# Low parts of second weight halves made by accumulating transfers

## The chip, the core and the metric

The kernel runs on one core of a Trainium2 chip. The time is device microseconds of one execution; the kernel before was timed twice, and 426.48 us is the median of the two (426.15 and 426.8). A profiled execution of its own gives the trace that is read below. "Within 2%" of the median is 418.0 to 435.0 us.

## The reference

One pre-norm residual layer on 512 tokens of width 1024, in float32, with two parallel token mixers that share one input projection:

```
h = rmsnorm(x, norm_g)
(q_lat, c_kv, k_rope, z_a, q_b, k_b, v_b, z_b,
 q_idx, k_idx, w_idx, gate_a, gate_b) = split(h @ w_in)
y_a = latent_attention(q_lat, c_kv, k_rope) * silu(z_a)      # 8 heads, chunk-causal softmax
y_b = topk_attention(q_b, k_b, v_b, q_idx, ...) * silu(z_b)  # 8 heads, an indexer keeps 128 keys
merged = sigmoid(gate_a) * (y_a @ w_o_a) + sigmoid(gate_b) * (y_b @ w_o_b)
x = x + merged @ w_out
return rmsnorm(x, final_g)
```

Nearly all the work is matrix products of activations with weights that are read once from HBM.

## The kernel before

**Products in three terms.** Every float32 operand `v` of a product is held as two tiles of the matmul type fp32r: a high part `hi`, which is `v` rounded to that type, and a low part `lo = v - hi`. A product of two such pairs is three matmuls, `hi*hi`, `hi*lo` and `lo*hi` (`mm3`, line 443; the matmul itself is recorded at line 438). A weight tile therefore costs, before TensorE can use it, a cast on ScalarE (line 331) and a subtraction on VectorE (line 362) or GpSimd (line 364).

**Jobs.** The projections are a list of jobs, in the order of the table `QUEUE`. One job loads one raw weight block into one of four buffers `raw0` to `raw3` (128 partitions, up to 1024 floats, 512 KB), and multiplies it. Three threads walk through the list: `fetcher` issues the load on SyncE's queue (line 465) as soon as a raw buffer is free; `splitter` makes the high and low parts, one half of 512 columns after the other (`split_w`); `multiplier` issues the matmuls, into accumulators of which at most three may be held by products at one time. `ga0` to `ga7`, `gb6`, `gb7` (gates), `za0` to `zb3` (SiLU paths) and the blocks `w_kb` and `w_qb` of `sb0` to `sb3` (keys and queries of the second mixer) are jobs of two halves of 512 columns each: 26 jobs. Names in capitals in the table go through a Strassen-like scheme and split their weights elsewhere.

**Slots.** High and low parts live in slots of 128x512 floats. `WCAP` bounds how many slots the class `w` may hold at one time: 8, that is, four halves. A half's two slots come free when TensorE has read them for the last time. The early weights of `early_w` (the key-value latent and the indexer, line 665 on) are under the same bound.

**The planner.** The order on each engine is not written out. `Flow` (line 151 on) runs while the program is built: some fifty threads (jobs, heads, softmaxes) each offer one step; the planner holds an estimate of each step's length and of each tile's readiness, and takes the step that would start first, ties and near ties going by priority. A step of `BOTH` engines goes to VectorE or GpSimd, whichever would end first. So an edit of one step's engine or estimate moves the order of everything behind it. Each engine then executes its own list strictly in order, and a wait holds up all that stands behind it. `multiplier` has the last priority but one (`PFILL`): its products fill TensorE between the steps of the attention heads.

**Heads.** A head's logits are four tiles of 128, 256, 384 and 512 keys (lines 1532 to 1534, three matmuls each, in the first mixer), written into two accumulator banks in turn (class `lg`, at most two held). A bank is free for the next tile when VectorE has taken its row maxima (line 1517) and ScalarE its exponentials with their sums (line 340). Softmax scaling, transposes (line 455) and the product with the values follow. The operands of the logits are put together by small transfers on SyncE's queue (`qhi`, `s_op`).

**GpSimd's own queue of transfers** (`pool_dma`, line 469) carries constants and small tables only, 15 transfers in the first 80 us.

Of the kernel before, what the change touches and what calls it, by code (L numbers as in the profile page):

```python
# [14 lines left out]
AF = mybir.ActivationFunctionType  # L15
ALU = mybir.AluOpType
# [4 lines left out]
S = 512  # L21
# [118 lines left out]
def put(*bufs):  # L140
    for b in bufs:
        b.home.used[b.cls] -= 1
        b.home.free.append(b)
# [7 lines left out]
class Flow:  # L151
# [16 lines left out]
    def spawn(self, gen, prio):  # L168
        t = Thread(gen, prio)
        self.threads.append(t)  # L170
        self.advance(t, None)
        return t
# [107 lines left out]
def tile_block(ctx: ExitStack, tc: tile.TileContext, a: dict, out: bass.AP, bias_dram: bass.AP):  # L280
    nc = tc.nc
# [28 lines left out]
    def in_ps(v):  # L310
        return id(v.buf) in ps_bufs

    def slot(cls, cap=None):
        return Get(SB, cls, cap)
# [8 lines left out]
    def bufs(*vs):  # L323
        return [v.buf for v in vs if isinstance(v, View)]
# [19 lines left out]
    def act(dst, src, func=AF.Copy, scale=None, bias=None, accum=None):  # L344
        step = Step([act_opt(dst, src, func, scale, bias, accum)], bufs(dst, accum), bufs(src, scale, bias))
        step.count = 2 if accum is not None else 1
        return step

    def rounded_by_dve(dst, src):
        step = Step([("DVE", 0.1 + 0.00052 * src.n, lambda: nc.vector.tensor_copy(dst.ap, src.ap))], bufs(dst), bufs(src))  # L350
        step.pair = True
        return step

    def soon(step):
        step.pbias = 0.0
        return step

    def tt(dst, x, y, op, engs=("DVE",)):
        opts = []
        for e in engs:  # L360
            if e == "DVE":
                opts.append(("DVE", 0.07 + 0.00104 * x.n, lambda: nc.vector.tensor_tensor(dst.ap, x.ap, y.ap, op=op)))  # L362
            else:
                opts.append(("POOL", 0.15 + 0.0021 * x.n, lambda: nc.gpsimd.tensor_tensor(dst.ap, x.ap, y.ap, op=op)))  # L364
        step = Step(opts, bufs(dst), bufs(x, y))
        step.pair = not (in_ps(x) or in_ps(y))
        return step
# [48 lines left out]
    def lo_part(lo, x, hi, engs=BOTH):  # L416

        return tt(lo, x, hi.f, ALU.subtract, ("DVE",) if in_ps(x) else engs)
# [48 lines left out]
    def pool_dma(dst, src):  # L467
# [3 lines left out]
        step.moves = 4.0 * dst.n * dst.ap.shape[0] / 360000  # L471
        yield step

    def act_dma(dst, src):
        step = Step([("ACT", 0.06, lambda: nc.scalar.dma_start(dst.ap, src))], bufs(dst), [])
        step.moves = 4.0 * dst.n * dst.ap.shape[0] / 360000
        return step
# [158 lines left out]

    rbc = []

    def split_w(raw, w, dst, key, cls="w", cap=None, release=False, early=False):

        hi = yield slot(cls, cap)
        lo = yield slot(cls, cap)
        yield rounded_by_dve(hi[:, :w], raw) if key == FIRST and early else act(hi[:, :w], raw)
        step = lo_part(lo[:, :w], raw, hi[:, :w])
        yield soon(step) if early else step
        if release:
            put(raw.buf)
        dst[key] = (hi, lo)
# [16 lines left out]
    def early_w():  # L665
        for k in range(NK):
            yield Until(lambda: ("q", k) in eraw)
            raw, last = eraw["q", k]
            yield from split_w(raw, 256, ewq, k if k else FIRST, "w", WCAP, last, True)
            if k == 0:  # L670
                ewq[0] = ewq.pop(FIRST)
            yield Until(lambda: ("kv", k) in eraw)
            raw, last = eraw["kv", k]
            yield from split_w(raw, 328, ewkv, k, "w", WCAP, last, True)
        for k in range(NK):
# [184 lines left out]
    def topk(i):  # L860
# [11 lines left out]
        if i == NT - 1:  # L872

            flow.pbias = LATE

# [33 lines left out]
    class Job:  # L909
        def __init__(self, src, widths, body, cls="w", cap=None, prep=None):  # L910
            self.src, self.widths, self.body, self.raw, self.parts, self.cls, self.cap = src, widths, body, None, {}, cls, cap or WCAP
            self.prep = prep
            jobs.append(self)
# [11 lines left out]
    def splitter():  # L925
        for job in jobs:
            yield Until(lambda: job.raw is not None)
            if job.prep:
                if job.body:
                    yield from job.prep(job)  # L930
                else:
                    spawn(job.prep(job), 9)
                continue
            for p, w in enumerate(job.widths):
                o = sum(job.widths[:p])
                yield from split_w(job.raw[:, o : o + w], w, job.parts, p, job.cls, job.cap, p == len(job.widths) - 1)

    def multiplier():
        for job in jobs:
# [28 lines left out]
    def input_sums():  # L968

        yield Until(lambda: sums_due[0] in done)  # L970
        for k in range(4):
            f = []
            for i in (k, k + 4):
                if i in held:
                    f.append(held[i])
                    continue
                t = yield slot("tmp", TCAP)
                yield soon(tt(t.all.f, hT[i][0].all.f, hT[i][1].all.f, ALU.add, BOTH))
                f.append(t)
            x, y = (t.all.f for t in f)  # L980
            yield soon(tt(x[:, HI], x[:, LO], x[:, HI], ALU.subtract, BOTH))
            yield soon(tt(y[:, HI], y[:, HI], x[:, HI], ALU.subtract, BOTH))
            yield soon(tt(x[:, LO], y[:, HI], x[:, LO], ALU.add, BOTH))
            yield soon(tt(y[:, LO], y[:, LO], y[:, HI], ALU.subtract, BOTH))
            for i in range(2):
                hi = yield slot("hs")
                lo = yield slot("hs")
                yield act(hi.all, f[i].all.f)
                yield soon(lo_part(lo.all, f[i].all.f, hi.all))
                put(f[i])  # L990
                hs[k, i] = (hi, lo)
# [434 lines left out]
    class Pair:  # L1426
# [3 lines left out]
        w = property(lambda self: max(self.hi.w, self.lo.w))  # L1430
# [209 lines left out]
    def y_gate(br, j):  # L1640

        name = "w_za" if br == "a" else "w_zb"
        y = ya if br == "a" else yb
        yield Until(lambda: (br, 2 * j) in done and (br, 2 * j + 1) in done and (name, j) in zt)
        z = zt[name, j]
        yield tt(y[j].all.f, y[j].all.f, z.all.f, ALU.mult, BOTH)
        put(z)
        yield is_done("pairs")
        hi = yield slot("ys")
        lo = yield slot("ys")  # L1650
        yield from split_scaled(hi.all, lo.all, y[j].all.f, 0.5)
        put(y[j])
        ysplit[br, j] = (hi, lo)
# [336 lines left out]
    spawn(bias_table(), 5)  # L1990
    spawn(fetcher(), 9)
    spawn(splitter(), 9)
    spawn(multiplier(), PFILL)
    spawn(setup_last(), 10)
# [5 lines left out]
    for br in "ab":  # L2000
        for j in range(4):
            spawn(y_gate(br, j), 8)
    spawn(input_sums(), PSUMS)
    spawn(fetch_gates(), 9)
# [12 lines left out]
XAT = 3  # L2017
QPOOL = 0
PHCAP = 4
WCAP = 8  # L2020
TCAP = 5
PTOPK = 12.0
PSCORE = 13.0
# [3 lines left out]
ORDER = [0,1,2,3]  # L2027
QUEUE = 'ga0 ga1 pe ma0 va0 ga2 za0 ma1 va1 ga3 za1 ma2 ga4 za2 ma3 ga5 za3 sb0 zb0 ga6 ga7 sb1 VB GB0 GB1 sb2 zb1 GB2 GB3 sb3 zb2 GB4 GB5 ou zb3 gb6 ou gb7 ou'
LATE = 0.75
PSUMS = 10.0  # L2030
PCAP = 9
BIAS_AT = 'kpe'
# [85 lines left out]
```

## Time and profile before

| | |
|---|---|
| median of the timed runs | 426.48 us (426.15, 426.8) |
| the profiled execution | 427.43 us, of which its instructions span 425.7 us |
| granted TensorE clock | 0.994 |
| TensorE matmuls busy, weight loads busy | 416.6 us (98%), 362.8 us (85%) |
| VectorE, ScalarE, GpSimd busy | 375.4 us (88%), 266.2 us (63%), 94.1 us (22%) |
| moved by transfers | 65.89 MB, mean 155 GB/s |

The profiled execution is 0.95 us over the median, and 1.73 us of it lie outside the span. Matmul busy time is counted until the modelled end of a pipelined matmul, so 98% does not say by itself that TensorE never waits. In the views, PE is TensorE's matmuls, PEld its weight loads, DVE VectorE, ACT ScalarE, POOL GpSimd, and SPq SyncE's queue. A row of the groups reads: line, engine, operation, output and inputs, shape, count; then busy time in us and the mean of one in ns; then the idle time of the engine before it, with what ended it.

### The profile page before, as it was taken

The page shows a single profiled execution, that of the slowest core. Times are in us where ns is not written, and L with a number is a line of the kernel's source. Part 1 is how long each engine was busy: PE and PEld are TensorE (multiplying, and loading weights), DVE is VectorE, ACT ScalarE, POOL GpSimd, SP SyncE. Part 2 cuts the span into 40 slices and gives each one's busy share as a digit, 9 for nine tenths or more (in the row PEclk, how much of TensorE's full clock was granted, in tenths as well). Part 3 has the DMA queues.
Part 4 walks back from the last instruction along what each step waited for, and adds up shares of the span by engine and source line. Part 5 has one row for each costly group of instructions (what it writes and reads, how often), then busy time and mean ns, then how long its engine had stood idle before and what let it go on. Part 6 is the DMA issues. An engine that isn't in the chain of part 4 may idle for free.

```text
span 425.7 us, 7077 instructions
## 1 busy us (share of the span) xinstructions
PE 416.6 (98%) x2305; PEld 362.8 (85%) x2305; DVE 375.4 (88%) x809; ACT 266.2 (63%) x597; POOL 94.1 (22%) x109
## 2 busy tenths in 40 slices
PE   8999999999999999999999999999999999999993
PEld 5999888798888888888899987998988888888883
DVE  4779899999989999999768899998699756999995
ACT  5787987367486947758354665584498534346625
POOL 1032548531435344220011001010030011000202
PEclk9999999999999999999999999999999999999997
DMA  8984433652444451654352444353452885557305
GB/s 261 395 282 122 123 111 106 195 155 49 148 133 147 122 169 49 159 152 125 101 166 68 158 155 110 92 162 105 101 186 68 267 330 196 179 167 256 123 0 197
DMA packets 30405, 65.89 MB, mean 155 GB/s; under 512 B 4648, under 2 KB 5944, under 8 KB 30368
## 3 DMA queue, kind: packets, MB, share of 16 engines
q1 hardware_dynamic: 29504, 64.21, 48.3%
q0 software_dynamic: 576, 0.83, 0.7%
q8 instruction: 18, 0.29, 0.3%
q10 hardware_dynamic: 288, 0.39, 0.3%
q14 instruction: 19, 0.16, 0.1%
HBM read 50.49 MB, written 4.21 MB: 129 GB/s over the span
## 4 chain that ended last, share of the span: by engine, by line
PE 70%; DVE 17%; ACT 4%; issue 3%; DMA 3%; SPq 1%; POOL 0%; POOLq 0%; DVEq 0%; ACTq 0%
PE ps L438 62%; PE ps L455 4%; ACT s_p L340 2%; DVE s_mg L362 1%; DVE s_wo L362 1%; PE ps L1533 1%; PE ps L1534 1%; DVE s_pair L362 1%; PE ps L1532 1%; DVE s_w L362 1%; SPq L465 1%; DVE s_xr L373 1%; DMA s_er<-w_kvl 1%; DVE s_wsum L362 1%; DVE s_pair L373 1%
## 5 line engine op out<-in xcount | busy, mean ns | idle before, releaser
L438 PE MATMUL ps<-s_h,s_w 128*128 128x512 f32 (+1 forms) x732 | 171.7, 380 | 0.0
L438 PEld LDWEIGHTS ps<-s_h,s_w 128*128 128x128 f32 x732 | 127.3, 189 | 21.5 <-issue 0.3
L331 ACT CAST s_w<-raw 128x512 fp32r<-128x512 f32 (+3 forms) x124 | 71.7, 592 | 28.7 <-DVE raw L362 9.5
L364 POOL TENSOR_TENSOR s_w<-raw,s_w 128x512 fp32r<-128x512 f32 (+2 forms) x39 | 47.9, 1236 | 143.5 <-ACT s_w L331 129.0
L362 DVE TENSOR_TENSOR s_w<-raw,s_w 128x512 fp32r<-128x512 f32 (+2 forms) x85 | 54.7, 659 | 5.7 <-ACT s_w L331 4.9
L438 PE MATMUL ps<-s_ys,s_w 128*128 128x512 f32 x192 | 43.7, 389 | 0.0
L438 PEld LDWEIGHTS ps<-s_ys,s_w 128*128 128x128 f32 x192 | 36.0, 188 | 7.5
L340 ACT ACTIVATE s_p<-s_p,sm 128x512 f32<-128x512 f32 (+3 forms) x56 | 31.1, 574 | 3.7 <-DVE sm L1614 3.3
L438 PE MATMUL ps<-s_w,s_xg 128*128 128x328 f32 (+1 forms) x192 | 33.0, 325 | 0.3 <-ACT s_rbc L331 0.2
L438 PE MATMUL ps<-s_wo,s_mg 128*128 128x512 f32 (+1 forms) x156 | 33.0, 373 | 0.0
L438 PEld LDWEIGHTS ps<-s_w,s_xg 128*128 128x128 f32 x192 | 31.4, 188 | 1.1 <-ACT s_rbc L331 0.5
L438 PEld LDWEIGHTS ps<-s_wo,s_mg 128*128 128x128 f32 x156 | 27.6, 188 | 5.2
L868 DVE MATCH_REPLACE8 mask<-sm,mask 128x256 f32<-128x256 f32 (+2 forms) x48 | 25.8, 540 | 0.0
L867 DVE MAX8 sm<-mask 128x8 f32<-128x256 f32 (+2 forms) x48 | 25.5, 548 | 0.2
L340 ACT ACTIVATE s_p<-ps,sm 128x128 f32<-128x128 f32 (+3 forms) x32 | 16.8, 526 | 13.8 <-DVE sm L1517 13.7
L455 PE MATMUL ps<-ident,s_p 128*128 128x128 f32 x160 | 22.9, 273 | 0.0
L455 PEld LDWEIGHTS ps<-ident,s_p 128*128 128x128 f32 x160 | 18.9, 140 | 3.0
L331 ACT COPY s_tmp<-ps 64x512 f32<-64x512 f32 (+1 forms) x18 | 10.2, 564 | 17.4 <-PE ps L438 15.7
L438 PE MATMUL ps<-s_hs,s_w 128*128 128x256 f32 x144 | 20.3, 285 | 0.0
L438 PE MATMUL ps<-s_lat,s_w 128*128 128x512 f32 x78 | 20.2, 392 | 0.0
L362 DVE TENSOR_TENSOR s_ph<-ps,s_ph 128x512 fp32r<-128x512 f32 (+1 forms) x32 | 18.7, 613 | 1.1 <-ACT s_ph L331 1.0
L331 ACT CAST s_ph<-ps 128x512 fp32r<-128x512 f32 (+1 forms) x32 | 15.8, 537 | 4.5 <-PE ps L455 4.4
(198 smaller groups left out, 752.3 us busy)
## 6 DMA issues: line engine op xcount, KB each, us to landing
raw<-w_out SPq DMA_DIRECT2D x18, 512.0 KB, 4.0
s_op<-s_op SPq DMA_DIRECT2D x36, 128.0 KB, 2.3
raw<-w_ga SPq DMA_DIRECT2D x8, 512.0 KB, 4.5
raw<-w_gb SPq DMA_DIRECT2D x8, 512.0 KB, 4.1
raw<-w_o SPq DMA_DIRECT2D x16, 256.0 KB, 3.3
s_x<-xT SPq DMA_DIRECT2D x8, 256.0 KB, 3.8
s_xn<-x SPq DMA_DIRECT2D x8, 256.0 KB, 6.5
bias_scratch<-s_sig SPq DMA_DIRECT2D x8, 256.0 KB, 2.9
```

Of the source, the lines that this page charges most:

```text
L331: nc.scalar.copy(dst.ap, src.ap)
L340: nc.scalar.activation(dst.ap, src.ap, func, **kw)
L362: opts.append(("DVE", 0.07 + 0.00104 * x.n, lambda: nc.vector.tensor_tensor(dst.ap, x.ap, y.ap, op=op)))
L364: opts.append(("POOL", 0.15 + 0.0021 * x.n, lambda: nc.gpsimd.tensor_tensor(dst.ap, x.ap, y.ap, op=op)))
L373: lambda: nc.vector.scalar_tensor_tensor(dst.ap, x.ap, sc(s), y.ap, op0=op0, op1=op1))],
L438: nc.tensor.matmul(ps.ap, l.ap, r.ap, start=start and i == 0, stop=stop and i == len(pairs) - 1, skip_group_check=more)
L455: nc.tensor.transpose(d.ap, s.ap, ident.tile)
L465: return Step([("SP", n / 360000.0, lambda: nc.sync.dma_start(d, s))], bufs(dst), bufs(src))
L867: yield Step([("DVE", t, lambda: nc.vector.max(m8.tile, work.tile))], [m8], [work])
L868: yield Step([("DVE", t + 0.068, lambda: nc.vector.match_replace(work.tile, m8.tile, work.tile, MARK))], [work], [m8])
L1532: nc.tensor.matmul(o, q0[0:100], k0[0:100], start=True, stop=False)
L1533: nc.tensor.matmul(o, q0[0:96], k1[0:96], start=False, stop=False)
```

## The change

Where a job's weights come as two halves of 512 columns, the low part of the second half is no longer a subtraction. ScalarE writes the negated high part into the low part's slot, and a transfer on GpSimd's queue adds the raw half to it while moving it from SBUF to SBUF. The raw buffer and the low part's slot are held until that transfer has landed. The planner charges the transfer with 0.53 us on GpSimd and adds `ADDED` = 2.0 to its landing. `WCAP` goes from 8 to 12.

```diff
+    def pool_add(dst, src):
+
+        step = Step([("POOL", 0.53, lambda: nc.gpsimd.dma_start(dst.ap, src.ap, accum_op=ALU.add))], bufs(dst), bufs(src, dst))
+        step.late = ADDED
+        step.moves = 4.0 * dst.n * dst.ap.shape[0] / 360000
+        yield step
+
...
-    def split_w(raw, w, dst, key, cls="w", cap=None, release=False, early=False):
+    def split_w(raw, w, dst, key, cls="w", cap=None, release=False, early=False, added=False):
 
         hi = yield slot(cls, cap)
         lo = yield slot(cls, cap)
         yield rounded_by_dve(hi[:, :w], raw) if key == FIRST and early else act(hi[:, :w], raw)
-        step = lo_part(lo[:, :w], raw, hi[:, :w])
-        yield soon(step) if early else step
+        if added and not early:
+            yield act(lo[:, :w], hi[:, :w].f, AF.Copy, scale=-1.0)
+            yield from pool_add(lo[:, :w].f, raw)
+        else:
+            step = lo_part(lo[:, :w], raw, hi[:, :w])
+            yield soon(step) if early else step
...
-                yield from split_w(job.raw[:, o : o + w], w, job.parts, p, job.cls, job.cap, p == len(job.widths) - 1)
+                yield from split_w(job.raw[:, o : o + w], w, job.parts, p, job.cls, job.cap, p == len(job.widths) - 1, added=p > 0 and w == S)
...
-WCAP = 8
+WCAP = 12
...
+ADDED = 2.0
```

Counted over the whole program, 26 such transfers and 26 negations on ScalarE appear. The 128x512 subtractions `s_w<-raw,s_w` go from 71 to 59 on VectorE and from 29 to 15 on GpSimd, those of 384 columns from 8 to 10 on VectorE and from 6 to 4 on GpSimd. Of the softmax scalings of `s_p`, eight more stand on VectorE, two of each width. TensorE's matmuls are the same, in another order.

In the rows below a number behind a name is that of the allocation, counted in the order in which the planner made it; two rows with one number speak of the same tile.

GpSimd's list in the middle of the first mixer, where it did nearly all low parts. Before:

```order
L364 TENSOR_TENSOR s_w_1753<-raw_68,s_w_1751 128x512
L395 TENSOR_SCALAR s_p_1688<-s_p_1688,sm_84 128x128
L364 TENSOR_TENSOR s_w_1805<-raw_69,s_w_1803 128x512
L364 TENSOR_TENSOR s_w_1823<-raw_69,s_w_1821 128x512
L395 TENSOR_SCALAR s_p_1744<-s_p_1744,sm_76 128x512
L364 TENSOR_TENSOR s_w_1878<-raw_66,s_w_1877 128x512
L364 TENSOR_TENSOR s_w_1946<-raw_66,s_w_1944 128x512
L364 TENSOR_TENSOR s_y_1905<-s_y_1905,s_z_1752 128x512
```

GpSimd's list at the same place now:

```order
L364 TENSOR_TENSOR s_w_1767<-raw_69,s_w_1766 128x512
L476 DMA s_w_1807<-raw_69 128x512
L395 TENSOR_SCALAR s_p_1770<-s_p_1770,sm_83 128x128
L364 TENSOR_TENSOR s_w_1854<-raw_67,s_w_1852 128x512
L476 DMA s_w_1889<-raw_67 128x512
L364 TENSOR_TENSOR s_w_1940<-raw_66,s_w_1939 128x512
L476 DMA s_w_1977<-raw_66 128x512
L364 TENSOR_TENSOR s_w_2010<-raw_68,s_w_2009 128x512
L476 DMA s_w_2030<-raw_68 128x512
```

Of the two halves of a raw buffer the first is still subtracted here, and the second has become a transfer.

SyncE's list just ahead of the first heads, with the semaphores that each row waits for (`DMASW` are GpSimd's transfers, `DMAHW` SyncE's). Before:

```order
L465 DMA bias_scratch<-s_sig_891 128x512 [waits DMAHW0_49,Activation_49]
L465 DMA raw_69<-w_va 128x512 [waits DMAHW3_49,DMAHW1_49,Pool_49]
L465 DMA qhi_72<-s_th_973 64x512 [waits DMAHW2_49,Activation_49]
L465 DMA qhi_73<-s_th_973 64x512
L465 DMA s_op_1005<-s_op_975 64x512 [waits DMAHW4_49,DVE_49,PE_49]
L465 DMA raw_66<-w_ga 128x1024 [waits DMAHW5_49,Pool_49]
L465 DMA qhi_73<-s_qpe_986 32x512 [waits DMAHW6_49,Activation_49]
```

SyncE's list there now:

```order
L465 DMA bias_scratch<-s_sig_902 128x512 [waits DMAHW1_49,Activation_49]
L465 DMA raw_67<-w_ga 128x1024 [waits DMAHW2_49,DMASW5_49,DMAHW4_49,Activation_49,Pool_49]
L465 DMA qhi_72<-s_th_985 64x512 [waits Activation_49]
L465 DMA qhi_73<-s_th_985 64x512
L465 DMA s_op_1013<-s_op_987 64x512 [waits DMAHW5_49,DVE_49,PE_49]
L465 DMA qhi_73<-s_qpe_972 32x512 [waits DMAHW6_49]
```

The load of a raw block that must wait for an accumulating transfer stands now ahead of the first moves for the first heads (`qhi`, `s_op`), where the like load stood behind them.

TensorE's list at the logits of the first two heads (lines 1532 to 1534; `ps` are accumulators, `s_h` and `s_lat` activations, `s_w` weights). Before, from the second tile of the first head on:

```order
L1532 MATMUL ps_94<-s_op_999,qhi_73 128x256
L1533 MATMUL ps_94<-s_op_1000,qhi_73 128x256
L1534 MATMUL ps_94<-s_op_999,s_op_975 128x256
L438 MATMUL ps_92<-s_h_662,s_w_1055 128x512
L438 MATMUL ps_92<-s_h_663,s_w_1055 128x512
L438 MATMUL ps_92<-s_h_662,s_w_1056 128x512
L438 MATMUL ps_96<-s_lat_810,s_w_1082 128x512
L438 MATMUL ps_96<-s_lat_811,s_w_1082 128x512
L438 MATMUL ps_96<-s_lat_810,s_w_1083 128x512
L1532 MATMUL ps_99<-s_op_999,qhi_73 128x384
```

Now, from the third tile of the first head (384 keys) to the second tile of the second head (the same lines are 1543 to 1545 in the changed file):

```order
L1543 MATMUL ps_95<-s_op_1005,qhi_73 128x384
L1544 MATMUL ps_95<-s_op_1006,qhi_73 128x384
L1545 MATMUL ps_95<-s_op_1005,s_op_987 128x384
L1543 MATMUL ps_92<-s_op_1005,qhi_73 128x512
L1544 MATMUL ps_92<-s_op_1006,qhi_73 128x512
L1545 MATMUL ps_92<-s_op_1005,s_op_987 128x512
L1543 MATMUL ps_99<-s_op_1041,qhi_72 128x128
L1544 MATMUL ps_99<-s_op_1090,qhi_72 128x128
L1545 MATMUL ps_99<-s_op_1041,s_op_1013 128x128
L1543 MATMUL ps_94<-s_op_1041,qhi_72 128x256
L1544 MATMUL ps_94<-s_op_1090,qhi_72 128x256
L1545 MATMUL ps_94<-s_op_1041,s_op_1013 128x256
```

Six matmuls of projections stood between every two tiles of the first head; now six tiles of the two heads, from 256 keys of the first to 384 of the second, follow each other with none between them. The first head's logits begin 19 rows later in TensorE's list than before.

## The prediction

> **What bounds the kernel now.** I read the page first (busy shares and the chain that ended last), then the busy times by stretch, then what TensorE waited for, and last the groups by shape that the change touches. From the page:
>
> ```profile
> PE 416.6 (98%) x2305; PEld 362.8 (85%) x2305; DVE 375.4 (88%) x809; ACT 266.2 (63%) x597; POOL 94.1 (22%) x109
> ...
> PE 70%; DVE 17%; ACT 4%; issue 3%; DMA 3%; SPq 1%; POOL 0%; POOLq 0%; DVEq 0%; ACTq 0%
> ```
>
> TensorE carries 70% of the chain and VectorE 17%. Whether TensorE is at its peak is not told by 98%, so the stretches are compared (us, then busy time and count of each engine, clock, DMA share, GB/s):
>
> ```profile
> 60.00:80.00 20.00, 20.00 (x101) 16.41 (x101) 19.65 (x40) 14.05 (x33) 14.20 (x16) 1.00 0.49 127
> ...
> 340.00:360.00 20.00, 20.00 (x90) 16.57 (x89) 11.62 (x19) 7.44 (x13) 2.59 (x2) 1.00 0.78 277
> 360.00:380.00 20.00, 20.00 (x89) 16.54 (x89) 19.72 (x33) 7.06 (x12) 1.48 (x2) 1.00 0.50 162
> ```
>
> The groups by shape say what the 340 to 380 us hold on TensorE, one row alone:
>
> ```profile
> L438 PE MATMUL ps<-s_ys,s_w 128*128 128x512 f32 x178 | 40.5, 389 | 0.0
> ```
>
> At 360 us 89 matmuls of 512 columns take 20 us: 225 ns each. The same rate holds at 340 us, where VectorE is busy for 11.62 us only. So these stretches run back to back on TensorE, with weight loads at 16.5 of 20 us, and VectorE, full in one and half idle in the other, makes no difference. At 60 us weight loads have the same density: there, too, TensorE is fed. What it does wait for (us in total, times, longest):
>
> ```profile
> PEld L541 <- issue: 1.9, 7, 0.3
> PEld ps L438 <- DVE s_ph L362: 1.7, 4, 0.5
> PEld ps L438 <- ACT s_xg L340: 1.3, 2, 0.8
> PEld L541 <- DVE neghalf L498: 1.0, 1, 1.0
> PEld ps L438 <- DVE s_last L362: 0.8, 3, 0.4
> PEld ps L1532 <- issue: 0.7, 1, 0.7
> ...
> PEld ps L894 <- issue: 0.4, 1, 0.4
> PE ps L1532 <- DMA s_op<-kpel: 0.3, 1, 0.3
> ```
>
> The ten PEld rows, from 1.9 down to 0.4, add up to 9.3 us, 2.9 of them in the warm-up at line 541. None names a weight part `s_w`: the low parts that the change moves are not waited for today. They can matter only through the engines that make them.
>
> **The change, part by part.** The rows that give its prices:
>
> ```profile
> L362 DVE TENSOR_TENSOR s_w<-raw,s_w 128x512 fp32r<-128x512 f32 x71 | 47.8, 685 | 4.8 <-ACT s_w L331 3.9
> L364 POOL TENSOR_TENSOR s_w<-raw,s_w 128x512 fp32r<-128x512 f32 x29 | 39.1, 1350 | 137.9 <-ACT s_w L331 128.3 <-PE ps L438 5.0 <-issue 2.5
> L362 DVE TENSOR_TENSOR s_w<-raw,s_w 128x384 fp32r<-128x384 f32 x8 | 3.9, 555 | 0.8 <-ACT s_w L331 0.8
> L392 DVE TENSOR_SCALAR s_p<-s_p,sm 128x384 f32<-128x384 f32 x7 | 3.9, 560 | 0.0
> L340 ACT ACTIVATE s_ys<-s_y 128x512 fp32r<-128x512 f32 x8 | 4.6, 631 | 1.4 <-DVE s_y L362 1.4
> L469 POOL DMA_DIRECT2D s_raw<-onehot x2: 534/546/557, 64.6 to 71.1; - x2
> ```
>
> *Subtractions removed.* VectorE loses 12 of 512 columns, 12 x 0.685 = 8.2 us, and gains two of 384 (1.1 us) and eight softmax scalings of at most about 0.56 us (4.5 us): net some -2.6 us of 375. GpSimd loses 14 x 1.35 = 18.9 us and gains 26 issues of 0.54 us, 14.0 us. Neither engine is waited for through a weight. What TensorE waits for VectorE's attention parts, `s_ph` and `s_last`, is 1.7 + 0.8 = 2.5 us, and that is all that a shorter queue on VectorE can give back. VectorE's relief is under 1% of its work, so I take 1.0 us, between 0 and 2.5.
>
> *Negations added.* 26 on ScalarE at the nearest row's 0.631 us make 16.4 us, 63% to 67% busy. TensorE's largest wait for ScalarE, 1.3 us for `s_xg`, belongs to the start, ahead of every negation; I take 0, with 1 us as the upper bound.
>
> *The transfers.* No accumulating transfer is in the trace. Rows for 256 KB or less (KB each, median us from issue to landing):
>
> ```profile
> s_op<-s_op SPq DMA_DIRECT2D x36, 128.0 KB, 2.3
> s_qs<-s_th SPq DMA_DIRECT2D x24, 48.0 KB, 2.0
> raw<-w_va SPq DMA_DIRECT2D x2, 256.0 KB, 2.8
> ropes<-ropes POOLq DMA_DIRECT2D x1, 256.0 KB, 6.2
> ```
>
> Within SBUF 80 KB more cost 0.3 us, so 256 KB cost about 1 us of data. A plain move of that size lands in 2.8 (SyncE's queue) to 6.2 us (GpSimd's, at 25 us, with the loads of the start in flight). The destination has to be read as well, at most another 1 us: 2.8 to 7.2 us, and I take 4.8, about the middle. The Trainium skill, "Collectives: The Full Stack", section "The bandwidth ceiling: the fold count and why AG ≠ RS ≠ AR", says that an add in the DMA engines is slow because it needs two source reads, which halves the rate. That agrees with the extra 1 us; no run here shows it yet.
>
> Cover: in the changed program I counted the matmuls that TensorE is handed between the place where the planner hands the transfer to GpSimd and the first matmul that reads its low part. At 225 ns per 512 columns that is 5.8 to 22.5 us; two transfers have 5.8, and five less than 8 (7.1, 7.6, 7.9 besides). At 4.8 us nothing is late. If all took 8 us, the five would miss by 2.2 + 2.2 + 0.9 + 0.4 + 0.1 = 5.8 us.
>
> *The held raw buffers.* SyncE's load of `raw_67` waits for a transfer and stands ahead of the first heads' moves. The count from that transfer's place to the first logits is over 20 us of matmuls, so a landing of 4.8 us is past long before.
>
> *The wider bound.* Six halves ahead instead of four: no wait for `s_w` exists that it could remove, also not in the first 35 us. I cost it at 0.
>
> *The order.* Here the change takes something. Six tiles of logits of the first two heads now follow each other without projections, and only two banks serve them. Per tile (the rows for 512 and 256 keys of VectorE's maxima and ScalarE's exponentials, and the sum's read-out):
>
> ```profile
> L1517 DVE TENSOR_REDUCE sm<-ps 128x1 f32<-128x512 f32 x8 | 5.4, 677 | 0.0
> L1517 DVE TENSOR_REDUCE sm<-ps 128x1 f32<-128x256 f32 x8 | 3.3, 407 | 0.0
> L340 ACT ACTIVATE s_p<-ps,sm 128x512 f32<-128x512 f32 x8 | 5.5, 694 | 0.5 <-DVE sm L1517 0.4
> L340 ACT ACTIVATE s_p<-ps,sm 128x256 f32<-128x256 f32 x8 | 3.7, 466 | 1.9 <-DVE sm L1517 1.9
> L340 ACT ACTIVATION_READ_ACCUMULATOR s_p<-ps,sm 128x1 f32 x32 | 6.3, 196 | 0.0
> ```
>
> A bank with 256 keys is free 0.407 + 0.466 + 0.196 = 1.07 us after its matmuls; the tile of 384 between covers 3 x 0.17 = 0.5 us (225 ns scaled to 384 columns), so TensorE waits about 0.55. A bank with 512 keys is free after 0.677 + 0.694 + 0.196 = 1.57 us, the tile of 128 between covers 0.3: 1.25 more. Together 1.8 us, where the place before has only the 0.7 and 0.3 us of line 1532. It is not below 0, and up to 4 us if VectorE, full there, takes the maxima late.
>
> **Sum.** 425.7 - 1.0 + 0 + 0 + 1.8 = 426.5 us of span. The profiled execution adds 1.73 us outside its span (427.43 in all) and lies 0.95 us over the median, so on the scale of the timed runs: 426.48 + 0.8 = **427.3 us**, no change that counts.
>
> **Rivals.**
> *VectorE is the bound, and relief there comes off the span.* For it: VectorE is the busiest by share of work after TensorE, 17% of the chain and 19.7 of 20 us at 360 us. The mechanism would be that the 12 subtractions of 8.2 us stood on its critical stretch: 426.48 - 8.2 = 418.3 us. Against it: TensorE's rate at 340 us, with VectorE half idle, is that at 360 us. The Trainium skill, "Perfetto Trace Analysis", section "Identifying the Most-Contended Engine", holds matmul busy time for a bad measure and judges TensorE by its weight loads' share. By that rule 85% would leave 63 us of headroom and VectorE's 88% would rank first. The trace does not agree: 83% of weight loads (16.54 of 20) is back to back here. Chance 0.06.
>
> *The transfers land late.* One mechanism: the read-modify-write of 256 KB lands after its first reader is due, and TensorE, in order, stands still for the rest. It decides from about 7 us on. At 10 us seven transfers miss by 17.4 us together (the five above, now by 2 us more each, and covers of 8.8 and 9.6): 443.9 us, slower. For it: the 6.2 us of `ropes` on the same queue, for a plain move. Against it: that ran amid the initial loads; issues at 64.6 and 71.1 us, where VectorE is 19.65 of 20 us busy, took 0.53 to 0.56 us, like any other. The Trainium skill, "SBUF — State Buffer", section "SBUF: two separate sides", warns that a VectorE copy in its two-port mode locks GpSimd out of writing descriptors, so that its transfers starve; by that rule this rival would be the likelier one. The 534 to 557 ns above do not show it. Chance 0.12.
>
> *The new order is worse in more places than one.* What costs 1.8 us at the first two heads recurs with other pairs, three or four times: 426.48 + 4 x 1.8 = 433.7 us, less the 1.0: 432.7. For it: all heads were planned anew. Against it: TensorE's waits at other heads sum to 2.5 us today. Chance 0.12.
>
> That the low parts stay on the path in another form is no separate case: the negation and the issue take their place inside the same cover.
>
> **Numbers.** The forecast has the chance 0.70, and alone reaches from 422 (all 2.5 us of waits gone, and 2 us at the heads' start) to 430 (4 us at the first heads). The third rival ends at 433, so 421.5 to 433 leaves out the late landings and the far end of the first rival. A measurement of this kernel tells about 2% from no change, 8.5 us. Faster by that: the first rival's better half, 0.03. Slower: late landings, most of 0.12, with a little of the third rival, 0.12. Within: 0.85.
>
> **What would show it.** Right: matmul counts of 89 or 90 per 20 us in the late stretches; waits of PEld still near 10 us in all, none over 1 us for `s_w`; a new wait of 1 to 3 us at lines 1543 to 1545 in the first two heads; landings of 3 to 6 us. Wrong: rows `PE` or `PEld` that wait for `s_w<-raw` transfers with some us in total (late landings), or a span below 420 with fewer waits on VectorE (first rival).

## The result, and the profile after

The changed kernel takes 430.78 us (two runs, 430.53 and 431.03) against 426.48 us: 1.0101 times the kernel before, with a 95% interval of 1.0058 to 1.0144. Timed again beside other kernels it gave 431.06 us against 426.76 us, 1.0111 (1.0094 to 1.0127). So it is 1% slower, within the 2% that was forecast as "no change that counts", and 3.5 us above the 427.3 us that the sum gave.

The profiled execution took 431.03 us with a span of 429.2 us, 3.5 us more than before. From its page, the busy times and the chain that ended last:

```profile
PE 417.9 (97%) x2305; PEld 364.3 (85%) x2305; DVE 372.1 (87%) x807; ACT 277.6 (65%) x619; POOL 95.4 (22%) x115
...
PE 87%; DVE 7%; DMA 2%; issue 1%; SPq 1%; ACT 0%; POOL 0%; POOLq 0%
```

VectorE did lose work, 375.4 to 372.1 us, and ScalarE went to 65%. GpSimd did not become lighter: 94.1 us before, 95.4 now. The groups of the changed operations (busy us, mean ns of one) say why:

```profile
L362 DVE TENSOR_TENSOR s_w<-raw,s_w 128x512 fp32r<-128x512 f32 x59 | 40.3, 697 | 7.1 <-ACT s_w L331 6.9
L476 POOL DMA_DIRECT2D s_w<-raw x26 | 23.2, 894 | 84.2 <-ACT s_w L340 53.2 <-PE ps L438 16.7 <-issue 5.6
L364 POOL TENSOR_TENSOR s_w<-raw,s_w 128x512 fp32r<-128x512 f32 x15 | 20.0, 1338 | 74.2 <-ACT s_w L331 72.2 <-DMA s_op<-s_qpe 1.0 <-POOL s_w L364 0.9
L340 ACT ACTIVATE s_w<-s_w 128x512 fp32r<-128x512 f32 x26 | 16.5, 636 | 0.4
```

The instructions on the raw buffers, GpSimd's alone, with the transfers' landing (ns and us, least, middle and most):

```profile
L476 POOL DMA_DIRECT2D s_w<-raw x26: 871/878/1113, 42.9 to 329.2; - x26
...
DMA to landing us min/median/max: 3.3/4.3/6.2
```

An accumulating transfer is busy on GpSimd for 0.89 us on average, where the plain ones of before took 0.54 us. What stands behind it starts sooner, though. GpSimd's list at 64 us:

```profile
64.46 0.94 POOL L476 DMA_DIRECT2D s_w<-raw  x1 [2.49 <-ACT rbs L331]
65.05 0.93 POOL L469 DMA_DIRECT2D s_raw<-onehot  x1
```

0.59 us after the first starts the next. Landings are as estimated: 3.3 to 6.2 us, 4.3 in the middle.

What TensorE's weight loads wait for, first over the whole span:

```profile
PEld L548 <- issue: 1.9, 7, 0.3
PEld ps L1543 <- ACT s_p L340: 1.6, 3, 0.9
PEld ps L438 <- ACT s_xg L340: 1.1, 2, 0.7
PEld L548 <- DVE neghalf L505: 1.0, 1, 1.0
PEld ps L1543 <- DMA s_op<-kpeh: 0.8, 1, 0.8
PEld ps L1543 <- DVE s_op L373: 0.8, 1, 0.8
```

With the three rows below them (0.5, 0.4, 0.4 us) they make 8.5 us, less than the 9.3 of before. None names a transfer of a weight. Gone are the rows for VectorE's `s_ph` and `s_last`, 2.5 us together. New are those of line 1543, the logits: 1.6 + 0.8 us at the first two heads, and 0.8 us at 163 us. By these rows alone the kernel would not be slower. The loss shows only when the clock is read beside them. Busy time and counts in four stretches of 2 us at the first two heads, the granted clock third from the end:

```profile
90.00:92.00 2.00, 1.46 (x6) 0.69 (x5) 2.00 (x7) 0.46 (x2) 0.00 (x0) 1.00 0.90 167
92.00:94.00 2.00, 1.30 (x7) 1.05 (x6) 2.00 (x7) 1.11 (x4) 0.00 (x0) 0.85 0.76 263
94.00:96.00 2.00, 2.00 (x8) 1.83 (x8) 2.00 (x9) 2.00 (x8) 1.28 (x2) 0.50 0.22 54
96.00:98.00 2.00, 2.00 (x15) 2.00 (x15) 2.00 (x7) 2.00 (x7) 1.48 (x3) 0.80 0.34 82
```

TensorE idles 0.54 + 0.70 us in the first two stretches, and then its clock is at half: 0.3 + 1 + 0.4 us of full speed are missing from 92 to 98 us, so 3.4 us at half the clock, some 1.7 us lost. From 94 to 96 us TensorE counts as busy all the time and does 8 matmuls. The idle time comes in three pieces (start and length of the matmul in us, and at the end the idle time before it with what ended it):

```profile
91.06 0.50 PE L1543 MATMUL ps<-s_op,qhi 100*128 100x512 f32 x1 [0.54 <-ACT s_p L340]
92.35 0.33 PE L1543 MATMUL ps<-s_op,qhi 100*128 100x128 f32 x1 [0.32 <-DVE s_op L373]
93.28 0.50 PE L1543 MATMUL ps<-s_op,qhi 100*128 100x256 f32 x1 [0.38 <-ACT s_p L340]
```

The first and the third are waits for an accumulator bank, the second is one for an operand that VectorE makes. Before, TensorE was busy at a clock of 1.00 here:

```profile
92.00:94.00 2.00, 2.00 (x18) 2.00 (x18) 2.00 (x9) 1.66 (x6) 1.72 (x3) 1.00 0.80 148
94.00:96.00 2.00, 2.00 (x16) 1.89 (x15) 2.00 (x7) 1.55 (x5) 0.03 (x1) 1.00 0.65 246
```

The other part is at the end. TensorE's last matmul ended at 418.8 us before and at 420.7 us now; the rest of the span behind it went from 6.9 to 8.5 us. VectorE's last rows (start, us, count), of the kernel after:

```profile
407.93 2.38 DVE L362 TENSOR_TENSOR s_part<-s_part,s_part 128x512 f32<-128x512 f32 x2
410.24 3.69 DVE L362 TENSOR_TENSOR s_xr<-s_xr,s_part 128x512 f32<-128x512 f32 x6
...
422.62 0.42 DVE L373 SCALAR_TENSOR_TENSOR s_xr<-ps,s_xr 128x256 f32<-128x256 f32 x1
```

Of the kernel before:

```profile
407.86 1.88 DVE L362 TENSOR_TENSOR s_xr<-s_xr,s_part 128x512 f32<-128x512 f32 x3
...
419.04 0.42 DVE L373 SCALAR_TENSOR_TENSOR s_xr<-ps,s_xr 128x256 f32<-128x256 f32 x1
```

VectorE read the last product 0.2 us after TensorE's end before, and 1.9 us after it now: it runs behind in the output stage.

So the profiled 3.5 us are 1.9 us on TensorE's side and 1.6 us at the end. Two explanations stand against each other. *Order*: the new order brought the waits, and the transfers are harmless. *Transfers*: their landings, their held buffers and their traffic cost the time, and the order is only where it shows.

### The profile page after: what moved, and what is told of

Its sections match the earlier page's. It is cut to its first block, busy times and chain, and to the rows that moved or that the text cites. A ratio compares the mean times of both kernels' runs of the same rounds, so it can differ in the third digit from the quotient of the medians.

```text
span 429.2 us, 7154 instructions
## 1 busy us (share of the span) xinstructions
PE 417.9 (97%) x2305; PEld 364.3 (85%) x2305; DVE 372.1 (87%) x807; ACT 277.6 (65%) x619; POOL 95.4 (22%) x115
## 4 chain that ended last, share of the span: by engine, by line
PE 87%; DVE 7%; DMA 2%; issue 1%; SPq 1%; ACT 0%; POOL 0%; POOLq 0%
PE ps L438 77%; PE ps L455 5%; DVE mask L879 1%; PE ps L1543 1%; PE ps L1544 1%; DVE sm L878 1%; DMA s_op<-s_op 1%; PE ps L1545 1%; PE ps L856 1%; PE ps L548 1%; DMA s_op<-kpeh 1%; DVE s_xr L373 1%; DVE s_rg L362 1%; SPq L465 1%; DVE s_xr L362 1%
## 5 line engine op out<-in xcount | busy, mean ns | idle before, releaser
L362 DVE TENSOR_TENSOR s_w<-raw,s_w 128x512 fp32r<-128x512 f32 (+2 forms) x75 | 48.3, 662 | 8.9 <-ACT s_w L331 8.6
L364 POOL TENSOR_TENSOR s_w<-raw,s_w 128x512 fp32r<-128x512 f32 (+2 forms) x23 | 27.6, 1217 | 88.9 <-ACT s_w L331 80.1
L476 POOL DMA_DIRECT2D s_w<-raw x26 | 23.2, 894 | 84.2 <-ACT s_w L340 53.2
L340 ACT ACTIVATE s_p<-s_p,sm 128x384 f32<-128x384 f32 (+3 forms) x52 | 28.7, 572 | 6.3 <-DVE sm L1625 5.8
L438 PEld LDWEIGHTS ps<-s_hs,s_w 128*128 128x128 f32 x144 | 18.6, 191 | 0.1
```

Of the source, the lines that this page charges most:

```text
L340: nc.scalar.activation(dst.ap, src.ap, func, **kw)
L438: nc.tensor.matmul(ps.ap, l.ap, r.ap, start=start and i == 0, stop=stop and i == len(pairs) - 1, skip_group_check=more)
L476: step = Step([("POOL", 0.53, lambda: nc.gpsimd.dma_start(dst.ap, src.ap, accum_op=ALU.add))], bufs(dst), bufs(src, dst))
```

## The experiments

Ratios are to runs of the kernel before that were made beside each kernel, medians of 426.5 to 426.8 us.

**Same order, no data.** The changed kernel with `dst.ap[:, :8], src.ap[:, :8]` in place of the whole half:

```diff
-nc.gpsimd.dma_start(dst.ap, src.ap, accum_op=ALU.add)
+nc.gpsimd.dma_start(dst.ap[:, :8], src.ap[:, :8], accum_op=ALU.add)
```

> The changed kernel, same order on every engine, but each of the 26 accumulating transfers moves 8 of the 512 columns (the rest of these low parts stays the negated high part, so that part of the computation is left out). The issue on GpSimd and the wait of the raw buffer stay; 6.5 of 6.6 MB that were read, added and written go. Theory 'order' (the loss stands in the new order: waits at the first heads, the clock that falls after them, VectorE late at the end): 429.5 to 431.5 us, with the granted clock at 0.5 for about 3 us after 93 us. Rival 'transfers' (the traffic and the landings cost the time): 426 to 427.5 us, and no dip of the clock. Between, 428 to 429: both have a part.

Measured: 429.74 us, 1.0066 (1.0051 to 1.0081). So 3.0 of the 4.3 us are there without the data, and 1.3 us come with it: both theories have a part. The waits at the first heads are the same (1.9 + 0.8 us on line 1543; TensorE idles 0.68 + 0.82 us from 90 to 94 us, a little more than above), but the profiled execution, at 428.06 us the fastest of six, had the clock at 1.00 all along:

```profile
92.00:94.00 2.00, 1.18 (x7) 0.83 (x7) 2.00 (x7) 1.29 (x5) 0.00 (x0) 1.00 0.69 223
```

Then the moves. Transfers and their landings, of the changed kernel:

```profile
s_w<-raw POOLq DMA_DIRECT2D x26, 256.0 KB, 4.3
...
s_op<-s_op SPq DMA_DIRECT2D x36, 128.0 KB, 2.9
...
raw<-w_o SPq DMA_DIRECT2D x16, 256.0 KB, 5.0
```

And of this one:

```profile
s_op<-s_op SPq DMA_DIRECT2D x36, 128.0 KB, 2.3
...
raw<-w_o SPq DMA_DIRECT2D x16, 256.0 KB, 3.4
...
s_w<-raw POOLq DMA_DIRECT2D x26, 4.0 KB, 2.6
```

By these rows the heads' operands land 0.6 us later with the data moving. A second profile of the changed kernel (below) has 2.4 us in the middle, so the difference is clearer by stretch: from 60 to 130 us 2.8 and 2.6 us in the two profiles with the data and 2.3 without, from 130 to 200 us 3.8 and 3.4 against 3.3. The rows of `raw<-w_o` say nothing about the transfers, though they differ by 1.6 us: the last transfer is issued at 329.2 us, 13 of the 16 loads come after 335 us (11 in the kernel with small transfers), and there the middle is 4.1 us in both. TensorE's wait at 163 us, for such an operand (`s_op<-kpeh`), is gone here, and the end behind the last matmul is 7.25 us in place of 8.5. An issue is busy for 878 ns in the middle, for 4 KB as for 256 KB.

Small transfers also land sooner, so the raw buffers are held for less time: SyncE waits 34.2 us for weight transfers, against 50.0 in the changed kernel. What the data costs can be its traffic or this longer holding; the run does not tell them apart.

**Old order, with transfers.** The kernel before, its order on TensorE and SyncE unchanged; at the place of 22 subtractions stand a negation and a transfer:

```diff
+        if added and len(seen) not in (6, 8, 18, 25):
+            def emit():
+                nc.scalar.activation(lo[:, :w].ap, hi[:, :w].f.ap, AF.Copy, scale=-1.0)
+                nc.gpsimd.dma_start(lo[:, :w].f.ap, raw.ap, accum_op=ALU.add)
+            step.options = [(e, t, emit) for e, t, _ in step.options]
```

> The kernel before, planned as before, so that TensorE's and SyncE's lists are those of the kernel before word for word; but 22 of the 26 second halves are made by negation on ScalarE and accumulating transfer at the place where their subtraction stood (the other four, whose first reader comes within 1.5 to 4.5 us of matmuls, stay subtractions). Theory 'order': 425 to 427 us, like the kernel before or a little better, no dip of the clock at 93 us. Rival 'transfers': 429 to 431 us, with waits for landings or for the moves of the heads' operands. Above 431: the old order leaves the transfers too little cover, and TensorE names a transfer of a weight as what it waits for.

Measured: 449.36 us, 1.0530 (1.0501 to 1.0559). Both ranges are missed, and the third reading fails too: TensorE names no transfer of a weight as what it waits for. The old order does not protect the kernel. What the transfers cost in it is the raw buffers that they hold. What SyncE's queue waited for most (us, times, longest):

```profile
SPq L465 <- DMA s_w<-raw: 101.9, 18, 9.5
```

SyncE's list around 190 us:

```profile
189.22 0.63 SPq L465 DMA_DIRECT2D qhi<-qhi  x1
195.02 0.34 SPq L465 DMA_DIRECT2D raw<-w_vb  x1
195.46 0.67 SPq L465 DMA_DIRECT2D qhi<-s_op  x1
```

TensorE behind it:

```profile
201.39 1.20 PE L438 MATMUL ps<-s_op,qhi 128*128 128x128 f32 x4 [5.68 <-DMA qhi<-s_op]
```

And the next stretches, with the clock:

```profile
202.00:204.00 2.00, 2.00 (x8) 1.71 (x8) 1.33 (x5) 1.41 (x5) 0.00 (x0) 0.50 0.00 0
204.00:206.00 2.00, 2.00 (x6) 1.62 (x5) 1.17 (x3) 1.05 (x4) 0.00 (x0) 0.50 0.00 0
```

The load of `raw<-w_vb` must wait until a transfer has read its raw buffer; SyncE stands still for 5.1 us, the operand `qhi` of the next head stands behind the load, and TensorE waits 5.7 us for that operand and then works at half the clock. At 84 and 160 us TensorE stands still for 1.9 and 2.0 us at the logits, the second time for such an operand (for the first the profile names none), after SyncE stood 3.9 and 3.3 us before loads of raw blocks; half a clock follows both times.

**The buffer freed.** To tell the held buffer from landing and traffic, the same kernel with another source of the same size:

```diff
-                nc.gpsimd.dma_start(lo[:, :w].f.ap, raw.ap, accum_op=ALU.add)
+                nc.gpsimd.dma_start(lo[:, :w].f.ap, hi[:, :w].f.ap, accum_op=ALU.add)
```

> The kernel in the old order with 22 transfers (449.4 us), with one operand changed: the transfer adds the high part and not the raw half (so these low parts become zero: that part of the computation is left out). Size, queue, place and landing of the transfers stay; but nothing holds the raw buffers until the landing, so SyncE's next load does not wait for it, nor the moves that stand behind that load. Theory 'held raw buffers': 427 to 430 us, and SyncE's 102 us of waits for weight transfers gone. Rival 'landing or traffic': 446 to 450 us, as before.

Measured: 434.35 us, 1.0177 (1.0163 to 1.0191). Of the 22.6 us over the kernel before, 14.8 were the held raw buffers. The other 7.8 us stay, so the expectation of 430 at most was too low: two landings are late, at 77 us (1.3 us for the weight load) and at 188 us, where a head's operand is late too and a half clock follows. What TensorE waited for from 180 to 200 us:

```profile
PE ps L438 <- DMA qhi<-s_op: 1.9, 1, 1.9
PE ps L438 <- DMA s_w<-s_w: 1.9, 1, 1.9
```

The landing did not stay as it was, as the expectation had it: 5.1 us in the middle, against 3.5 us with the buffers held. So the 14.8 us are what is left after landings that came later. Why they came later is open. The buffers are also free a little sooner than in the kernel before, where a subtraction still read them.

**The wider bound alone, and the transfers without it.** First the kernel before with `WCAP = 12`, then the changed kernel with `WCAP = 8`.

> The kernel before with the bound on weight slots at 12 instead of 8, and nothing else; all low parts are subtractions. The planner makes an order of its own again. Theory 'order': any order that the planner makes anew moves some 1 to 5 us either way; 424 to 431 us. If it gives 430 us or more with bunched logits at the first heads, the wider bound alone is the cause; at 426 to 427 it is not.

> The changed kernel with the bound on weight slots back at 8: all 26 transfers stay, in yet another order, with less cover (3.4 us at the least, four under 6 us). Theory 'order': 425 to 431 us, by where the logits fall; waits for transfers of weights under 1.5 us in all. Rival 'transfers': 430 to 433 us, as they are all still there, the covers shorter.

Measured: 429.19 us, 1.0065 (1.0044 to 1.0086), and 436.94 us, 1.0227 (1.0199 to 1.0256). Without one transfer the wider bound makes an order that is 2.4 us slower. In its profiled execution (431.37 us, the slowest of its six) the waits are others (1.0 us for `s_op` at 92 us, 1.3 us for `s_last` and `s_ph` at 317 us), and the end is late like that of the changed kernel, 8.5 us behind the last matmul. With the transfers it is the other way round: eight slots take 5.9 us more than twelve (436.94 against 431.06), above both ranges. That is yet another order too, so how much of it is the bound is not shown. There SyncE waits 67.7 us for weight transfers, against 50.0 in the changed kernel, and TensorE up to 1.8 us at a time for a head's operand, with a half clock at 197 us.

**The changed kernel once more**, without an edit.

> The changed kernel as it is, once more, so that it stands beside the same runs of the kernel before as the next three, and for how far its own executions spread. If the half clock after the waits at the first heads comes in some executions and not in others, as the run with small transfers has it (428.06 us without, 429.1 to 430.7 in the others), the times spread over some 2 us, and an execution at 428 to 429 us has no dip near 93 us. If the dip is in every one: 430 to 431.5 us, all alike.

Measured: 431.06 us (429.37 to 432.64 in five). The profiled one, the fastest of the five, took 429.37 us: 1.3 + 0.8 us on line 1543 at the first heads, 1.1 us at 163 us, no half clock. The stretch where the other profile had it:

```profile
91.00:93.00 2.00, 1.40 (x6) 0.77 (x6) 2.00 (x7) 0.53 (x2) 0.00 (x0) 1.00 0.87 241
93.00:95.00 2.00, 1.64 (x10) 1.44 (x11) 2.00 (x8) 1.77 (x6) 0.48 (x1) 1.00 0.52 146
95.00:97.00 2.00, 2.00 (x18) 1.98 (x17) 2.00 (x8) 2.00 (x9) 2.00 (x4) 1.00 0.19 46
```

Two profiles of one kernel, 431.03 us with the dip and 429.37 us without, are 1.7 us apart, the half of 3.4. In part that is chance: TensorE's last matmul ends only 1.0 us later with the dip (420.7 against 419.7 us), and its other waits differ too. The other executions left no trace, but their granted clock is on record: 0.996 at 429.37 us and 0.997 at 428.06 us of the run without data, and 0.986 to 0.993 in the eleven other executions of the two kernels, 429.1 to 432.6 us. A dip of 3.4 us lowers the mean by 0.004. So most executions of this order very likely have at least one, and the two fastest have none.

The two profiles without a dip are 1.3 us apart (429.37 and 428.06), which is what the data costs by the medians too. Of this 0.7 us are TensorE's wait at 163 us, and 0.6 us the end behind the last matmul, 7.9 us against 7.25.

**Transfers away from the first heads.** Transfers and the wider bound from the 15th job on (18 transfers), and the same bound without transfers (parts of the changed lines; the early weights keep the bound of 8):

```diff
-cls, cap or WCAP
+cls, cap or (WCAP if len(jobs) >= 14 else 8)
...
-added=p > 0 and w == S)
+added=p > 0 and w == S and 14 <= jobs.index(job) < 99)
```

> The changed kernel with transfers and the wider bound only from the 15th job of the list on (18 transfers of 26); what is ahead, the first two heads among it, is planned as before, up to about 125 us. Theory 'order': the waits at the first heads, the half clock behind them and the 0.6 us at 163 us go: 426 to 428 us, the rest being VectorE behind at the end (0 to 1.6 us). Rival 'transfers': two thirds of them are still there, so two thirds of the loss: 429 to 429.5 us.

> The kernel before with the wider bound from the 15th job on and no transfer at all: the partner of the run with the late transfers. If both have the same time, the transfers themselves cost nothing there; if this one has 426 to 427 us and that one 428 or more, they do. If both stand 1 to 2 us over the kernel before and end with VectorE behind TensorE, the wider bound makes the end late.

Measured: 426.68 us, 1.0014 (0.9991 to 1.0037), and 426.50 us, 1.0008 (0.9994 to 1.0021). Eighteen transfers in a fitting order, with the work that they take off, cost nothing that can be told, and gain nothing either.

**All transfers, another order.** The planner told what the profile shows of a transfer (parts of the changed lines):

```diff
-Step([("POOL", 0.53, lambda: nc.gpsimd.dma_start(dst.ap, src.ap, accum_op=ALU.add))]
+Step([("POOL", 0.88, lambda: nc.gpsimd.dma_start(dst.ap, src.ap, accum_op=ALU.add))]
...
-ADDED = 2.0
+ADDED = 0.5
```

> The changed kernel, with the planner told what the trace shows of a transfer: 0.88 us of issue on GpSimd in place of 0.53, and an addition of 0.5 us to the landing in place of 2.0 (about 4.1 us from issue to landing, where 4.3 is the median). All 26 transfers and the wider bound stay; in the order that comes out, projections stand between the logits of the first two heads again. Theory 'order': no dip of the clock at 90 us, 426.5 to 429 us. Rival 'transfers': 430 to 432 us, since their number and size are the same and two of them have 4.0 and 4.5 us of cover alone.

Measured: 427.01 us, 1.0015 (0.9991 to 1.0038), as theory 'order' had it. All 26 transfers are in it, and 4.1 of the 4.3 us are gone by the medians. Its twelve executions spread from 425.2 to 431.4 us (the kernel before: 425.8 to 427.4), and the slowest has a granted clock of 0.987, so this order is not always without a dip. In the profiled one, at 427.74 us, TensorE is never idle from 80 to 100 us; first this kernel, then the changed one:

```profile
80.00:100.00 20.00, 20.00 (x110) 17.04 (x110) 19.51 (x59) 12.87 (x32) 5.56 (x8) 1.00 0.49 131
```

```profile
80.00:100.00 20.00, 18.76 (x93) 15.44 (x92) 19.00 (x62) 10.54 (x28) 4.79 (x8) 0.91 0.62 171
```

One wait for a landing came up in its profile, at 332 us, where a transfer with 5.9 us of cover took 6.7 us to land:

```profile
PE ps L438 <- DMA s_w<-raw: 1.4, 1, 1.4
```

**Its three nearest parts subtracted, and its data taken away.** The three transfers with the least cover become subtractions on GpSimd at their place; in the next kernel all 26 carry 8 columns, as in the first experiment.

```diff
+            near = len(seen) + 1 in (6, 25, 26)
...
+                if near:
+                    step.options = [(e, t, lambda: nc.gpsimd.tensor_tensor(lo[:, :w].ap, raw.ap, hi[:, :w].f.ap, op=ALU.subtract)) for e, t, _ in step.options]
```

> The kernel with the measured prices, in its order, but the three low parts with the least cover (4.0, 4.5 and 5.9 us of matmuls to their first reader) are subtracted on GpSimd at the place of their transfer, 23 transfers stay. Its profile showed one wait of TensorE for a transfer, 1.6 us at 332 us, at the third of these. Theory 'order': that wait goes, 425 to 426 us, below the kernel before by 0.2 to 0.4%. Rival 'transfers': nothing but three transfers less, 426.5 to 427 us. If 1.35 us of subtraction on GpSimd is late there as well: 427 us, with a wait for GpSimd in its place.

> The kernel with the measured prices, in its order, with transfers of 8 of 512 columns (the rest of these low parts stays the negated high part; that part of the computation is left out). Theory 'order': the data of the transfers costs only the one late landing, 425 to 426 us against 427.0. Rival 'transfers': their traffic slows the loads and the moves of the heads' operands all along, 424 us or less. If it stays at 427, the data costs nothing at all.

Measured: 426.83 us, 1.0012 (1.0000 to 1.0024), and 424.31 us, 0.9952 (0.9940 to 0.9964). The first lies in the range of the rival: the wait is gone from its profile, but the late landing was no steady cost, and taking it away changed nothing that can be told. The second lies between the two ranges. The data is a steady cost: 2.7 us by the medians (427.01 and 424.31), 2.5 us when each is taken against the kernel before beside it. The two profiles show where some of it is: the 1.4 us wait; the heads' operands (`s_op<-s_op`), which from 60 to 130 us land in 3.8 us against 2.4 and from 130 to 200 us in 3.4 against 2.3; an end behind the last matmul of 7.6 us against 7.0. The rest is not located, and here too the raw buffers are held for less time without the data (SyncE waits 55.9 us for weight transfers against 76.5). And 2.2 us below the kernel before is what this order with its fewer subtractions would be worth if moving the data were free.

**All 26 subtracted on GpSimd, same order.**

```diff
-            near = len(seen) + 1 in (6, 25, 26)
+            near = True
```

> The kernel with the measured prices, in its order, but all 26 low parts are subtracted on GpSimd at the place of their transfer (1.35 us of GpSimd in place of 0.88 us of issue and some 4 us of landing), and ScalarE's 26 negations go. No accumulating transfer is left, the wider bound and VectorE's lighter load stay. If what holds the kernel with the transfers at 427 us instead of 424.3 is their data: 424.3 to 425.5 us, faster than the kernel before by 0.2 to 0.5%. If the gain of the run with small transfers came from GpSimd's freed time: 427 us or more, as GpSimd's tensor operations share VectorE's way into SBUF and stretch both.

Measured: 430.71 us, 1.0087 (1.0073 to 1.0101), the second reading, and more of it than put: 6.4 us over the kernel with the small transfers. The busy times of its page, and then its first waits of weight loads that are not of the start:

```profile
PE 417.4 (97%) x2305; PEld 362.9 (85%) x2305; DVE 377.0 (88%) x806; ACT 264.0 (62%) x592; POOL 113.6 (26%) x117
```

```profile
PEld ps L455 <- DVE s_p L392: 2.3, 6, 0.8
PEld ps L438 <- DVE s_last L362: 2.2, 2, 1.7
```

Against the kernel with the small transfers, VectorE is busy 8.2 us more (368.8 there) for as many instructions: its 61 subtractions of 512 columns take 715 ns each in place of 685, its six scalings `s_p` of 256 columns 462 in place of 349, beside a GpSimd with 113.6 us of work in place of 99.5. TensorE waits for VectorE's attention parts again. So the transfers do relieve: in this order they are 3.7 us better than GpSimd's subtractions. That holds for an order that was planned for transfers. No kernel here that computes everything is faster than the kernel before by more than the noise.

## Why the prediction was right, and where its sum was short

The forecast, no change that counts, held: 1.0101 is within 2%, and 430.78 us lies in 421.5 to 433. But it lies above the 422 to 430 that the forecast had by itself, nearer to the 432.7 us of the third rival than to 427.3. Term by term:

- *The bound.* Right. The late stretches are as before, 90 matmuls in 20 us at 340 and at 360 us.
- *Subtractions removed, -1.0 us.* Right in kind, small in size. The 2.5 us of waits for `s_ph` and `s_last` all went, the outer end of the term's range. In the better order, with the data taken away, the kernel stands 2.2 us under the one before. On GpSimd the term was wrong: an issue put at 0.54 us is busy for 0.89, so GpSimd's 4.9 us of gain did not come. Nothing waited for it in the profile after.
- *Negations, 0.* 26 x 0.636 = 16.5 us beside other work; none was waited for.
- *Transfers' landing, 0 at 4.8 us.* Landings of 4.3 us and no wait for a weight: right. What failed is that a transfer was weighed only by who waits for its result. Moving the data is 1.3 us in this order and 2.5 to 2.7 in the better one, in part through heads' operands that land later. No term stood for it.
- *Held raw buffers, 0.* No wait of TensorE at the first heads was traced to them in this order, which was planned with the landing counted. In the old order, planned without it, they are the costliest thing here: 14.8 us.
- *The wider bound, 0.* Wrong taken alone, +2.4 us, though through the order and not through weights; and perhaps as a part, since the transfers without it take 5.9 us more in the order that comes out then.
- *The order, +1.8 us, not below 0 and up to 4.* The waits came where they were put, but shorter on TensorE: 0.54 us at the first bank, where 0.55 was put, and 0.70 us at the second, where 1.25 was put and 0.32 of the 0.70 was for an operand. The 0.3 us of idle TensorE that the place had before were to be taken off and were not. So the waits were not too low; what follows them was left out: 3.4 us at half the clock, 1.7 us in the executions that have it. No term stood for it either, nor for an end at which VectorE is late: behind the last matmul 8.5 us in one profile and 7.9 in the other, 8.5 with the bound alone, 6.9 before. The same order without the data has 7.25 us, so of this end 0.4 us are the order's and 0.6 to 1.2 us came with the data.

One execution shows the parts side by side. Without data and without a dip this order took 428.06 us, 0.8 us above the forecast's 427.3. The data (1.3 us) and the half clock (1.7 us), which the sum did not have, make up the rest. That the total still fell within 2% is what the prediction had right; that it fell within 421.5 to 433 is owed in part to a bound that was set for another mechanism, three or four bad pairs of heads.

The clock has a rule that the prediction did not use. The Trainium skill, "TensorE: Matmul & The Clock Gate", section "Part 1: The HAM clock gate (the "warmup" mystery)", tells of a free-running window of about 3.4 us after which the clock goes to half or back. The length agrees: 3.4 us at 94 us, and about twice that, 6.8 us, from 201 us in the old order. That one idle window is needed does not agree: ahead of the dip at 94 us TensorE was never idle for more than 0.54 us at a time. The Trainium skill's section "A second HAM failure mode: psum-queue depth-cycling" of the same page, on short idles between groups that go through the accumulator banks in turn, describes this place better.

By the rivals: VectorE as the bound (418.3 us) and late landings (443.9 us) both fell with the first profile. The third, a worse order in more places, names the order rightly, but there are not three or four such places: there is one place with its half clock, a wait of 0.8 us at 163 us that is gone without the data, and the end. That its 432.7 us lie nearer to the result is luck.

## What to carry to other kernels

Where a planner makes the order, a change of one kind of step has two prices, its own and that of the order that comes out; run the same order without the step's work, and the same work in another order, before either is blamed. A transfer that takes a copy off an engine still holds its source until it lands, and whatever stands behind the next load into that source pays; look at the queue of that load, not at the reader of the result. Read the clock beside short waits of TensorE that lie close together: here 1.2 us of them within 3 us were followed by 1.7 us lost at half the clock in one profiled execution, and 1.5 us of them by no loss of clock in another of the same order.

## What the runs showed that was not expected

- Half clock after short waits, and not every time. Three idle pieces of 0.32 to 0.54 us within 3 us brought 3.4 us at 0.50 in one profiled execution; the same pieces and one more of 0.28 us brought none in the profiled execution with small transfers. Single waits of about 2 us (84 and 160 us in the old order) were followed by it; single ones of 1.0 and 1.4 us (at 92 us with the wider bound alone; at 332 us with the measured prices) were not.
- The issue of an accumulating transfer is busy on GpSimd for 878 ns in the middle, for 4 KB and for 256 KB, but at 64 us the next instruction starts 0.59 us after it; a plain one of before, at the same time of the kernel, took 0.53 to 0.56 us, and 0.93 us directly behind an accumulating one.
- Accumulating 256 KB within SBUF lands 4.3 us after its issue in the middle, 4 KB after 2.6 us (the changed kernel and its order with small transfers).
